# Modulation sums on VectorE, half of the low parts by adding DMAs, and values transposed, in a transformer layer

## The chip, the cores and the metric

The kernel runs on one core of a Trainium2 chip. The metric is the time of one execution on the device in microseconds (us), as the median of three runs.

## What is computed

One layer for 512 tokens of width 2048, all in fp32: a modulation of norms and residuals by a vector c, a mixer of eight attention heads (each query keeps 128 keys, picked by an index score) and sixteen RWKV-7 heads, an output projection, and a gated feed-forward of width 5632.

```python
mod = silu(c) @ w_ada + b_ada
sh1, sc1, gt1, sh2, sc2, gt2 = split(mod, 6)
h = rms_norm(x, norm1_g) * (1 + sc1) + sh1
proj = h @ w_in
mixed = concat([attention(proj[..., :4176]), rwkv7(proj[..., 4176:])]) @ w_out
x = x + gt1 * mixed
h2 = rms_norm(x, norm2_g) * (1 + sc2) + sh2
x = x + gt2 * ((silu(h2 @ w_gate) * (h2 @ w_up)) @ w_down)
```

## The kernel before

**Products.** Activations lie transposed, features on the 128 partitions and tokens along the row, as tiles of 128x512. A large product is made of three, to keep fp32 accuracy: each operand is split into a rounded high part and a low part (what is left), and high x high, high x low and low x high are added up in PSUM.

**Weight stream.** All large products form one list of jobs. A job is one chunk of weights of 512 KB, loaded into `wraw` (three buffers), split in two halves into `whi` and `wlo` (four buffers each, 128x512), and used by 24 products of 128x512. ScalarE makes the high part by a copy into the rounded type, `split` then has the low part made by a subtraction. In the middle section of the list (`state["mid"]`, 110 jobs from the rest of the input projection's groups up to the output projection, about 155 to 1130 us) every second low part is made by GpSimd, the others by VectorE. `split_to` puts the splits of a chunk into the queues about one and a half chunks ahead of its products.

**Side work.** Everything else is written as generators that yield, and `drive` lets each go a step further after every third product, so that side work is laid between the products in TensorE's queue. Whether a step is ready is judged by a rough clock kept while the program is written (`clk`, one entry for each queue): `until` waits for that clock to pass the time at which a tile should be there, `room` for a queue's backlog to be small. On the chip each engine takes its queue in order; if an operand is later than the rough clock thought, TensorE stands still.

**RWKV.** `prep` (line 650), once for each of eight pairs of heads, makes decays and scaled keys with a chain on VectorE from the scan `L` to the tile `work`; `work` is stored, transposed by TensorE into the PSUM tile pT, and the values `vt` are turned into token-major form in the PSUM tile pV by products with the identity. Both are copied into `pack` by ScalarE, four chunks of 64 tokens in each of two halves, and stored. `solve` (line 779) solves the triangular systems of four pairs at a time, one problem on each partition; the first four on GpSimd, the second four on VectorE. A scan over the chunks and the attention heads follow.

**Modulation.** The first third of `mod` (shift and scale of the first norm) is made at the start. `ada_stream` (line 966) makes the other four vectors gt1, sh2, sc2 and gt2, each in four blocks of 512 columns: for each of 16 rows of blocks of w_ada a 256 KB tile `wad` comes in, ScalarE multiplies it by the column of silu(c), GpSimd adds it to the block's sum, and `ada_sum` adds up over the partitions. There are 256 such tiles; from the last four of the output projection's column tiles until the first gate tile the last vector's tiles are held back (`state["rest"]`). The output projection's end needs gt1, the second norm sh2 and sc2, the down projection gt2.

Of the kernel before, what the change touches and what calls it, by code (L numbers as in the profile page):

```python
# [8 lines left out]
F32 = mybir.dt.float32  # L9
# [9 lines left out]
KD = D // 128  # L19
# [21 lines left out]

# columns of the constant table
C_ID, C_MASK, C_CAUS, C_BLKM = 0, 128, 256, 384
# [5 lines left out]
def layer_kernel(ctx, tc, x, c, positions, w_ada, b_ada, norm1_g, w_in, q_norm_g, k_norm_g,  # L49
# [5 lines left out]

    # A rough clock for each queue, kept while the program is written: it decides when side work joins the queues.
    clk = dict(pe=0.0, dve=0.0, act=0.0, pool=0.0, dma=0.0)
# [77 lines left out]

    SLACK = 0.5

    def until(*aps):
        """let the products run on until what these hold is there."""
        t = max(ready.get(nm(a), 0.0) for a in aps) + SLACK  # L140
        while now() < t:
            yield
# [5 lines left out]
    def banks(n):  # L148
        """wait for n free banks of the side pool."""
        while True:  # L150
            for k in [k for k, v in psread.items() if v is not None and v <= now()]:
                del psread[k]
            if len(psread) + n <= 4 and side["pe"] <= SIDE:
                return
            yield
# [42 lines left out]

    # ---------------------------------------------------------------- constants
    cst = const.tile([128, C_W], F32, name="cst")  # L200
# [27 lines left out]

    # ---------------------------------------------------------------- weight stream
    jobs = []  # L230
    subs = []
    state = {"issued": 0, "split": 0, "mid": False, "rest": False}

    def job(view, k0, nk, c0, ncols, mms, need=None, before=None, after=None, whole=False):
        """a chunk of weights, with the products that use it; its two halves are split one by one."""
        j = dict(view=view, k0=k0, nk=nk, c0=c0, n=ncols, mms=mms, need=need, before=before, after=after, i=len(jobs),
                 hi=[], lo=[], s0=len(subs), whole=whole)
        jobs.append(j)
        subs.extend([(j, u) for u in range(min(nk, 2))])
# [9 lines left out]
    def split_to(n):  # L249
        while state["split"] < min(n, len(subs)):  # L250
            j, u = subs[state["split"]]
            if j["i"] >= state["issued"]:
                return
            h = max(1, j["nk"] // 2)
            hi = wpool.tile([128, 512], F32R, name="whi", tag="whi", bufs=4)
            lo = wpool.tile([128, 512], F32R, name="wlo", tag="wlo", bufs=4)
            hv, lv = (t[:, 0:h * j["n"]].rearrange("p (k m) -> p k m", m=j["n"]) for t in (hi, lo))
            split(hv, lv, j["raw"][:, u * h:(u + 1) * h], P if state["mid"] and state["split"] % 2 else V)
            j["hi"] += [hv[:, i, :] for i in range(h)]
            j["lo"] += [lv[:, i, :] for i in range(h)]  # L260
            state["split"] += 1
# [38 lines left out]
    def group_T(view, c0, mts, klist, kc, rhs, evac, pool=PG, need=None, before=None, kneed=None, add=True, chunk_done=None, apart=False):  # L300
        """out^T tiles: mts = [(column offset, M)], contracted over klist in chunks of kc."""
        box = {}
# [31 lines left out]

    # ---------------------------------------------------------------- inputs
    xtok = [[hpool.tile([128, 512], F32, name="xtok", tag="h") for _ in range(4)] for _ in range(NT)]
# [16 lines left out]

    # scale and shift, some columns at a time; the loads run as far ahead as there is room
    BLOCKS = [(0, 1), (1, 1)] + [(k, 2) for k in range(2, KD, 2)]
# [38 lines left out]

    # rms of x, and x transposed
    ssq = SM("ssq")
# [12 lines left out]

    # vectors as columns  # L410
    v1 = const.tile([128, 128], F32, name="v1")
# [25 lines left out]
    def tables():  # L437
        """cos and signed sin of the rotary angles, features on partitions."""
        pos = G("pos", I32)
# [32 lines left out]

    # first group: the loras and two tiles of k, as the columns of h come
    first = []
# [47 lines left out]

    # ---------------------------------------------------------------- modulation, first part
    def colsum(dst, t):
        """column 32 b + c of t, summed over the partitions of a quarter, to partition c of the quarter and column b."""
        u = G("tr")
        V.transpose(u, t)
        V.tensor_reduce(dst, u.rearrange("p (b c) -> p b c", c=32), axis=mybir.AxisListType.X, op=OP.add)

    def spread(ps, parts, col=C_MOD):  # L530
        """the quarters added up: the sum of column 128 j + q to partition q and column j."""
        pv = parts.rearrange("p (j a) -> p a j", a=4)
# [60 lines left out]

    # ---------------------------------------------------------------- rwkv: evacuation with token shift
    def shifted(ps, M, mcol, name):
# [33 lines left out]

    # scratch in DRAM  # L630
    pk = dram.tile([NC, 128, PAIRS, 512], F32, name="pk")
# [18 lines left out]
    def prep(j):  # L650
# [77 lines left out]
        for half in range(2):  # L728
# [4 lines left out]
            pV = PS("pV")  # L733
            for cc in range(4):
                cI = half * 4 + cc
                mm(pV[64:128, cc * 128:(cc + 1) * 128], vt[:, cI * C:(cI + 1) * C], ident)
            yield
            A.copy(pack[half][:, :, 256:384], pT.rearrange("p (c f) -> p c f", f=128))
            A.copy(pack[half][64:128, :, 384:512], pV[64:128].rearrange("p (c f) -> p c f", f=128))
            yield from banks(2)  # L740
# [34 lines left out]

    # ---------------------------------------------------------------- rwkv: triangular solve, one problem per partition
    solved = set()
# [42 lines left out]

    # ---------------------------------------------------------------- rwkv: chunk scan over all heads
    mix = {}
    scanned = set()

    def scan(g):
        """the pairs of a group, chunk after chunk."""
        while g not in solved or done["prep"] < PAIRS:
# [131 lines left out]

    # ---------------------------------------------------------------- modulation, second part  # L960
    mod = {n: const.tile([128, 16], F32, name=n) for n in ("gt1", "sh2", "sc2", "gt2")}
# [4 lines left out]
    def ada_stream():  # L966
# [11 lines left out]

        nl = ns = 0
        acc = None  # L980
        for i, (bi, k) in enumerate(chunks):
            while state["rest"] and bi >= 12:
                yield
            while nl < i + (4 if 0 not in mix else 2):
                load(nl)
                nl += 1
            while ns < min(i + 2, nl, len(chunks)):
                t = tiles[ns]
                if ns > i and ready[nm(t)] > now():
                    break  # L990
                yield from until(t)
                A.activation(t, t, AF.Copy, scale=ccol(chunks[ns][1]))
                ns += 1
            t = tiles.pop(i)
            if k == 0:
                acc = t
                continue
            yield from until(t)
            yield from room("pool", 1.0 if 0 < done["prep"] - 3 and 0 not in solved else 2.5)
            P.tensor_tensor(acc, acc, t, op=OP.add)  # L1000
            if k == KD - 1:
                start(ada_sum(acc, *blocks[bi]))
# [17 lines left out]

    # ---------------------------------------------------------------- attention
    iwt = const.tile([128, NT, 16], F32, name="iwt")
# [142 lines left out]

    # the four query tiles of a head share three banks
    PLACE = {3: (0, 0), 2: (1, 0), 0: (1, 384), 1: (2, 0)}
# [63 lines left out]

    # ---------------------------------------------------------------- the main stream of products
    ALLK = list(range(KD))
# [38 lines left out]

    # out projection, contracted over the rwkv half first
    mT = {}
# [34 lines left out]
    def evac_out(m0):  # L1309
        def f(ps, which=(0, 1)):  # L1310
            for i in which:
                m, p = m0 + i, ps[i]
                state["rest"] = m >= KD - 4
                t = xres.pop(m)
# [21 lines left out]
    for m in range(4, KD, 2):  # L1336
        group_T(wout, m * 128, TWO, KO, 4, mixed, evac_out(m), kneed=kneed, before=load_x([m, m + 1]),
                apart=m == KD - 2)
    # the column sums of the squares need every tile
    i_norm2 = len(jobs)  # L1340
# [3 lines left out]
    def norm2():  # L1344
# [15 lines left out]
        A.copy(rb2, prb)  # L1360
        att["rb2"] = rb2

    def h2make(k):
# [7 lines left out]

    # feed-forward, in parts of its width
    gate = {}
# [3 lines left out]
    def evac_gate(f0):  # L1377
        def f(ps):
            state["rest"] = False
            for i in range(2):  # L1380
# [41 lines left out]

    # gate and up together in the first group, as the columns of h2 come
    gbox, ubox = {}, {}
# [26 lines left out]

    # ---------------------------------------------------------------- go
    start(run_rb())
# [106 lines left out]
```

## Time and profile before

| | |
|---|---|
| time, median of 3 runs | 2809.06 us (2808.62 to 2809.23) |
| profiled execution | its span of 2808.0 us; no other time of it is listed |
| instructions | 35665 |
| mean granted TensorE clock | 0.975 |

The profile shows one execution, taken by the hardware profiler. PE is TensorE's products, PEld its weight loads, DVE VectorE, ACT ScalarE, POOL GpSimd, SP SyncE, which issues most DMAs. Every line of a group has the number L127, as all operations pass one helper; so groups are told apart by their tiles, written as output<-inputs. A granted clock of 1.00 stands for the upper of TensorE's two levels (2.4 GHz), the lower one is half of it. An fp32 product that is not split is listed as two records, a transpose as one.

### The profile page before, as it was taken

The numbers are of one execution on the slowest core, as the hardware profiler recorded it, in microseconds if no ns is written. First come the engines' busy times: TensorE is split into PE (matmuls) and PEld (weight loads), VectorE is DVE, ScalarE is ACT, GpSimd is POOL, SyncE is SP. The second block draws the span as 40 slices with busy tenths as digits, with TensorE's granted clock in tenths as the row PEclk, the third lists the DMA queues.
The fourth block names the chain that finished last, engine by engine and source line by source line (L and its number), as shares of the span: only waits on it lengthen the run. The fifth ranks groups of instructions, "written<-read, shape, count | busy, mean of one in ns | idle before, by whom it ended". The sixth has DMA issues, their size and how long they took to land.

```text
span 2808.0 us, 35665 instructions
## 1 busy us (share of the span) xinstructions
PE 2699.7 (96%) x13439; PEld 2131.3 (76%) x13439; DVE 1362.6 (49%) x2064; ACT 953.0 (34%) x1691; POOL 801.9 (29%) x695
## 2 busy tenths in 40 slices
PE   7998988988999999999799999999999999999999
PEld 4576766667677768788688888888888888888887
DVE  4476445588957875743743233232333323333333
ACT  3255542332333335554452222222222222222222
POOL 2057768974434566654340000000000000000000
PEclk8999999989999999999899999999999999999999
DMA  9976765355466434464253333323333333333233
GB/s 324 312 243 202 227 184 146 103 131 174 149 198 195 137 128 136 156 220 149 77 193 98 98 98 97 97 95 96 97 98 98 98 98 98 98 98 95 93 101 110
DMA packets 383580, 396.12 MB, mean 141 GB/s; under 512 B 52442, under 2 KB 332832, under 8 KB 383408
## 3 DMA queue, kind: packets, MB, share of 16 engines
q1 hardware_dynamic: 381312, 387.78, 44.5%
q0 software_dynamic: 1952, 5.81, 0.6%
q8 instruction: 105, 1.72, 0.3%
q14 instruction: 67, 0.55, 0.1%
q10 hardware_dynamic: 144, 0.26, 0.0%
HBM read 358.13 MB, written 35.65 MB: 140 GB/s over the span
## 4 chain that ended last, share of the span: by engine, by line
PE 81%; DVE 9%; DMA 4%; POOL 2%; issue 2%; ACT 1%; SPq 1%; DVEq 0%; ACTq 0%; POOLq 0%
PE acc L127 71%; DMA wraw<-in_w_in_dram 2%; PE p L127 1%; DVE X L127 1%; PE po L127 1%; DVE stmp L127 1%; PE vacc L127 1%; DVE work L127 1%; DVE wlo L127 1%; SPq L127 1%; PE adaacc L127 1%; DMA wada<-in_w_ada_dram 1%; DVE score L127 1%; PE pV L127 1%; DVE u L127 0%
## 5 line engine op out<-in xcount | busy, mean ns | idle before, releaser
L127 DVE TENSOR_TENSOR wlo<-wraw,whi 128x512 fp32r<-128x512 f32 (+2 forms) x750 | 553.2, 743 | 1111.3 <-ACT whi L127 1104.8
L127 ACT CAST whi<-wraw 128x512 fp32r<-128x512 f32 (+2 forms) x860 | 517.9, 607 | 1251.9 <-PE acc L127 1085.7
L127 PE MATMUL acc<-hhi,whi 128*128 128x512 f32 (+1 forms) x2256 | 914.4, 405 | 4.4 <-ACT hhi L127 4.0
L127 PE MATMUL acc<-hhi,wlo 128*128 128x512 f32 (+1 forms) x2256 | 887.2, 393 | 19.2 <-DVE wlo L127 15.5
L127 PE MATMUL acc<-hlo,whi 128*128 128x512 f32 (+1 forms) x2256 | 886.2, 393 | 3.6 <-DVE hlo L127 3.6
L127 PEld LDWEIGHTS acc<-hhi,whi 128*128 128x128 f32 (+1 forms) x2256 | 425.2, 188 | 128.4 <-issue 32.4
L127 PEld LDWEIGHTS acc<-hhi,wlo 128*128 128x128 f32 (+1 forms) x2256 | 426.0, 189 | 116.3 <-DVE wlo L127 19.3
L127 PEld LDWEIGHTS acc<-hlo,whi 128*128 128x128 f32 (+1 forms) x2256 | 426.3, 189 | 95.4 <-DVE hlo L127 6.4
L127 PE MATMUL acc<-act,whi 128*128 128x512 f32 x1408 | 434.8, 390 | 0.0
L127 POOL TENSOR_TENSOR wad<-wad 128x512 f32<-128x512 f32 x240 | 343.0, 1429 | 150.5 <-ACT wad L127 139.0
L127 PEld LDWEIGHTS acc<-act,whi 128*128 128x128 f32 x1408 | 263.2, 188 | 53.8
L127 PE MATMUL acc<-act,wlo 128*128 128x512 f32 x704 | 274.0, 389 | 0.0
L127 POOL TENSOR_TENSOR wlo<-wraw,whi 128x512 fp32r<-128x512 f32 (+1 forms) x110 | 157.9, 1436 | 235.4 <-ACT whi L127 223.9
L127 ACT ACTIVATE wad<-wad,cact 128x512 f32<-128x512 f32 x256 | 179.0, 719 | 14.4 <-DMA wad<-in_w_ada_dram 14.1
L127 PEld LDWEIGHTS acc<-act,wlo 128*128 128x128 f32 x704 | 132.1, 188 | 27.6
L127 PE MATMUL acc<-mhi,whi 128*128 128x512 f32 x256 | 100.5, 392 | 0.0
L127 PE MATMUL acc<-mhi,wlo 128*128 128x512 f32 x256 | 99.7, 389 | 0.0
L127 PE MATMUL acc<-mlo,whi 128*128 128x512 f32 x256 | 99.6, 389 | 0.0
L127 DVE SCALAR_TENSOR_TENSOR x<-acc,gt,x 128x512 f32<-128x512 f32 x80 | 57.3, 750 | 41.6 <-PE acc L127 41.6
L127 POOL TENSOR_TENSOR X<-X,stmp 128x504 f32<-128x504 f32 (+33 forms) x69 | 67.0, 970 | 5.4
L127 POOL TENSOR_TENSOR stmp<-X,N 128x504 f32<-128x504 f32 (+33 forms) x69 | 63.7, 923 | 4.6 <-DVE work L127 1.4
L127 PE MATMUL vacc<-whi,hhi 128*128 128x512 f32 x128 | 58.1, 454 | 0.0
(257 smaller groups left out, 2328.5 us busy)
## 6 DMA issues: line engine op xcount, KB each, us to landing
wad<-in_w_ada_dram SPq DMA_DIRECT2D x256, 256.0 KB, 4.4
wraw<-in_w_in_dram SPq DMA_DIRECT2D x108, 512.0 KB, 5.0
wraw<-in_w_ffn_down_dram SPq DMA_DIRECT2D x88, 512.0 KB, 3.4
wraw<-in_w_ffn_gate_dram SPq DMA_DIRECT2D x84, 512.0 KB, 3.5
wraw<-in_w_ffn_up_dram SPq DMA_DIRECT2D x84, 512.0 KB, 3.4
wada<-in_w_ada_dram SPq DMA_DIRECT2D x128, 256.0 KB, 6.7
wraw<-in_w_out_dram SPq DMA_DIRECT2D x32, 512.0 KB, 3.5
pk<-pack SPq DMA_DIRECT2D x16, 768.0 KB, 3.8
```

The source lines that it names most:

```text
L127: return f(*args, **kw)
```

## The change

- **Modulation's second part.** ScalarE scales only the first of a block's 16 tiles. The other 15 are multiplied and added in one instruction on VectorE (240 in all, `scalar_tensor_tensor`, both tensors in SBUF). A step comes not before 4.2 us by the rough clock after the last one (3.0 us for the last vector), and loads run three tiles ahead at most. The last vector's tiles wait until the second norm is done (`state["ffn"]`), so they run beside the feed-forward; `state["rest"]` is gone.
- **Low parts.** In the middle section every second low part, which GpSimd made, comes about in another way: ScalarE writes the negated high part into `wlo`, and a DMA issued by GpSimd reads the same 256 KB of weights from DRAM again and adds them to it.
- **Values transposed.** In `prep`, per half, four products of 64 columns with the identity become two transposes of 128 columns; the copies into `pack` are two instead of one, each with every second chunk.

The lines of the diff that only drop a comment are left out.

```diff
+    PACE, PACE2 = 4.2, 3.0
...
-    state = {"issued": 0, "split": 0, "mid": False, "rest": False}
+    state = {"issued": 0, "split": 0, "mid": False, "ffn": False}
...
-            split(hv, lv, j["raw"][:, u * h:(u + 1) * h], P if state["mid"] and state["split"] % 2 else V)
+            if state["mid"] and state["split"] % 2:
+                A.copy(hv, j["raw"][:, u * h:(u + 1) * h])
+                A.activation(lv, hv.bitcast(F32), AF.Copy, scale=-1.0)
+                P.dma_start(lv, j["view"][:, j["k0"] + u * h:j["k0"] + u * h + h, j["c0"]:j["c0"] + j["n"]],
+                            accum_op=OP.add)
+            else:
+                split(hv, lv, j["raw"][:, u * h:(u + 1) * h])
...
             pV = PS("pV")
-            for cc in range(4):
-                cI = half * 4 + cc
-                mm(pV[64:128, cc * 128:(cc + 1) * 128], vt[:, cI * C:(cI + 1) * C], ident)
+            for i in range(2):
+                tb = half * 2 + i
+                PE.transpose(pV[:, i * 128:(i + 1) * 128], vt[:, tb * 128:(tb + 1) * 128], ident)
             yield
             A.copy(pack[half][:, :, 256:384], pT.rearrange("p (c f) -> p c f", f=128))
-            A.copy(pack[half][64:128, :, 384:512], pV[64:128].rearrange("p (c f) -> p c f", f=128))
+            for odd in range(2):
+                A.copy(pack[half][64:128, odd::2, 384:512], pV[odd * 64:odd * 64 + 64, 0:256].rearrange("p (i f) -> p i f", f=128))
...
-        nl = ns = 0
+        nl = 0
         acc = None
+        last = 0.0
         for i, (bi, k) in enumerate(chunks):
-            while state["rest"] and bi >= 12:
+            while bi >= 12 and not state["ffn"]:
                 yield
-            while nl < i + (4 if 0 not in mix else 2):
+            while nl < min(i + 3, 192 if bi < 12 else 256):
                 load(nl)
                 nl += 1
-            while ns < min(i + 2, nl, len(chunks)):
-                t = tiles[ns]
-                if ns > i and ready[nm(t)] > now():
-                    break
-                yield from until(t)
-                A.activation(t, t, AF.Copy, scale=ccol(chunks[ns][1]))
-                ns += 1
             t = tiles.pop(i)
+            while now() < last + (PACE if bi < 12 else PACE2):
+                yield
+            yield from until(t)
+            yield from room("dve", 2.0)
+            last = now()
             if k == 0:
+                A.activation(t, t, AF.Copy, scale=ccol(0))
                 acc = t
                 continue
-            yield from until(t)
-            yield from room("pool", 1.0 if 0 < done["prep"] - 3 and 0 not in solved else 2.5)
-            P.tensor_tensor(acc, acc, t, op=OP.add)
+            V.scalar_tensor_tensor(acc, t, ccol(k), acc, op0=OP.mult, op1=OP.add)
...
-                state["rest"] = m >= KD - 4
...
         att["rb2"] = rb2
+        state["ffn"] = True
...
-            state["rest"] = False
```

## Rows read from the trace of the kernel before

**Rows 1.** The page's part 1: busy us, share of the span, instructions.

```profile
PE 2699.7 (96%) x13439; PEld 2131.3 (76%) x13439; DVE 1362.6 (49%) x2064; ACT 953.0 (34%) x1691; POOL 801.9 (29%) x695
```

**Rows 2.** By stretch: length, busy PE PEld DVE ACT POOL, clock, DMA share, GB/s.

```profile
200.00:400.00 200.00, 177.68 (x909) 135.83 (x908) 110.09 (x119) 98.18 (x164) 147.86 (x110) 0.94 0.71 215
400.00:600.00 200.00, 176.33 (x871) 128.86 (x870) 118.24 (x135) 61.66 (x113) 166.21 (x160) 0.91 0.44 122
600.00:800.00 200.00, 183.25 (x976) 134.98 (x975) 167.27 (x238) 64.20 (x122) 91.26 (x85) 0.91 0.61 170
...
1360.00:1380.00 20.00, 17.91 (x69) 14.33 (x70) 17.90 (x28) 7.21 (x15) 7.23 (x5) 0.86 0.26 79
1400.00:1620.00 220.00, 220.00 (x978) 181.94 (x977) 77.51 (x108) 79.13 (x131) 34.03 (x26) 1.00 0.39 129
```

**Rows 3.** Waits of PE in 200:400, 400:600, 600:800: us, times, longest.

```profile
PE pT L127 <- DVE work L127: 21.1, 4, 5.9
...
PE pT L127 <- DVE work L127: 15.1, 3, 7.1
...
PE acc L127 <- DVE wlo L127: 7.1, 3, 3.7
```

**Rows 4.** DVE in order of time, 305 to 345: start, duration, operation.

```profile
313.38 2.32 DVE L127 TENSOR_TENSOR_SCAN L<-reset,sg 128x512 f32<-128x512 f32 x1
...
322.18 1.75 DVE L127 TENSOR_TENSOR at<-at,e 128x512 f32<-128x512 f32 x1
...
325.52 1.74 DVE L127 TENSOR_TENSOR work<-kf,e 128x512 f32<-128x512 f32 x1
```

**Rows 5.** Operations on the tile ang: count, ns least/median/most, first and last start.

```profile
L127 DVE SCALAR_TENSOR_TENSOR ang<-nrot,ang x8: 681/1666/1775, 163.0 to 183.6; 128x512 f32<-128x512 f32 x8
```

**Rows 6.** POOL in order of time, 305 to 345.

```profile
312.83 1.79 POOL L127 TENSOR_TENSOR wlo<-wraw,whi 128x512 fp32r<-128x512 f32 x1
...
328.36 6.13 POOL L127 TENSOR_TENSOR wad<-wad 128x512 f32<-128x512 f32 x4
```

**Rows 7.** PE in order of time, 318 to 340; in brackets the wait before.

```profile
327.32 1.11 PE L127 MATMUL pT<-cst,work 128*128 128x128 f32 x4 [5.03 <-DVE work L127]
328.37 1.97 PE L127 MATMUL pV<-cst,v 128*64 128x128 f32 x8
...
333.63 0.60 PE L127 MATMUL pT<-cst,work 128*128 128x128 f32 x4
334.16 1.09 PE L127 MATMUL pV<-cst,v 128*64 128x128 f32 x8
335.18 0.50 PE L127 MATMUL acc<-hhi,whi 128*128 128x512 f32 x1
```

**Rows 8.** Groups of instructions in 155:1130: busy us, mean ns, idle before.

```profile
L127 POOL TENSOR_TENSOR wad<-wad 128x512 f32<-128x512 f32 x161 | 232.8, 1446 | 38.3 <-ACT wad L127 30.3 <-PE vacc L127 2.2
L127 POOL TENSOR_TENSOR wlo<-wraw,whi 128x512 fp32r<-128x512 f32 (+1 forms) x108 | 154.6, 1432 | 235.3 <-ACT whi L127 223.9 <-PE pst L127 11.1
L127 ACT CAST whi<-wraw 128x512 fp32r<-128x512 f32 (+1 forms) x217 | 131.8, 615 | 242.4 <-DMA wraw<-in_w_in_dram 103.8 <-PE acc L127 102.6 <-PE vacc L127 23.4
L127 ACT ACTIVATE wad<-wad,cact 128x512 f32<-128x512 f32 x174 | 120.9, 719 | 14.4 <-DMA wad<-in_w_ada_dram 14.1
```

**Rows 9.** By stretch: the solve's stmp (DVE, POOL), then PE's products with whi.

```profile
400.00:450.00 50.00, 0.00 (x0) 27.85 (x36) 0.97 0.46 127
...
150.00:200.00 50.00, 44.90 (x147) 1.00 0.81 278
...
1050.00:1100.00 50.00, 36.73 (x117) 1.00 0.39 127
...
155.00:1130.00 975.00, 572.06 (x1716) 0.95 0.56 169
```

**Rows 10.** DMA issues: KB each, median us from issue to landing.

```profile
wad<-in_w_ada_dram SPq DMA_DIRECT2D x256, 256.0 KB, 4.4
...
wraw<-in_w_in_dram POOLq DMA_DIRECT2D x7, 256.0 KB, 6.3
```

## Prediction

> **What bounds the kernel now.** First the page's head: TensorE is busy 96% of the 2808.0 us, VectorE 49%, ScalarE 34%, GpSimd 29% [rows 1]. Time can only be won where TensorE waits or runs at the lower clock, or by giving TensorE less to do.
>
> Next the busy time by stretch [rows 2], to see where the missing 4% lie. TensorE lacks 22.3 us in 200 to 400, 23.7 in 400 to 600 and 16.8 in 600 to 800, with a mean granted clock of 0.94, 0.91 and 0.91; in the feed-forward from 1400 on it is full at 1.00. All that the change touches, except the last vector, lies between 155 and 1130 us.
>
> Then the waits of TensorE [rows 3]. Up to 600 us nearly all is one wait: the transposes pT wait for VectorE's `work`, 21.1 us in four waits and then 15.1 in three. From 600 to 800 the largest is for low parts from VectorE, 7.1.
>
> Last, one such wait in order of time. VectorE's chain from `L` at 313.38 to the last `work` ends at 327.26 [rows 4]. Five of its operations have two inputs in SBUF, 128x512 or 128x504, and take 1.64 to 1.77 us each (two of them are shown); a multiply-add of this size takes 0.68 us at its shortest, with a median of 1.67 [rows 5]. GpSimd works without a gap through just that time, making `wlo` and adding up `wad`; the first and the last of six such groups are shown [rows 6]. On TensorE [rows 7] the wait is 5.03 us, and what follows runs at the lower of the clock's levels: four transposes take 1.11 us where the next four take 0.60, the eight pV records 1.97 where the next eight take 1.09.
>
> **The change part by part.**
>
> *Values transposed.* Each half of a pair has eight pV records now; from pV to the next product is 1.02 us at full clock (334.16 to 335.18), against 0.53 from four pT to pV (333.63 to 334.16) [rows 7]. Two transposes should thus take 0.27 us: 0.75 saved, 16 times, 12.0 us of TensorE. Part of it may fall into a wait, so the bounds are 0 and 12.0; I take 12.0, since this work stands behind the wait, not in it. ScalarE's one evacuation becomes two of half the length; if each took a cast's 0.62 us [rows 8], that would be 10 us more in all on an engine that is busy 98 of 200 us at most here [rows 2]: hidden.
>
> *Vector sums on VectorE.* Gone are ScalarE's scaling of `wad` (0.72 us each) and GpSimd's adds (1.45 us each) [rows 8]; 240 multiply-adds with two SBUF inputs come to VectorE, and 16 scalings stay. One costs 0.68 us alone and up to 1.77 against GpSimd [rows 5]; with GpSimd's two big readers gone I take 0.7. At one in 4.2 us or more that is 33 us in 200, hidden wherever VectorE has that room: it has 90, 82 and 33 us free in the three stretches [rows 2]. Where it has not, all of it delays the chain.
>
> Between 200 and 400 GpSimd's readers were these two, so the chain's five slow operations fall from about 1.71 to 0.69: 5.1 us less, as long as the wait was (5.03); `L`, 2.32 us beside GpSimd, should fall too and pay for one multiply-add in between. So I let the waits of this stretch go, 22.3 us, and with each of the four the slow work behind it, about 2.1 us (1.11 less 0.60, 1.97 less 1.09, some 0.7 in the products after): 30.7 in all. Bounds: 15, if half stays, and 34, if the clock recovers wholly (6% of 200 us).
>
> Between 400 and 600 the first solve runs on GpSimd, 27.9 us of the first 50 [rows 9], and goes on reading SBUF. What leaves GpSimd here is a fifth of the 154.6 us of low parts, 31 us [rows 8]; what comes to VectorE is 33 us. The chain then gains little: I take 5 us, between a loss of 21 (the 15.1 us of waits doubled, and 6 of slow clock) and a gain of 30 (all 23.7 idle, and 6 of clock).
>
> Between 600 and 800 the second solve is on VectorE, slowed by GpSimd's `wad` and `wlo`. Against 33 us more stand most of GpSimd's 91 us, gone [rows 2]. I take half of the 16.8 us idle, with some clock 9; bounds 0 and 23. Next late there is the scan, which goes from TensorE to ScalarE and VectorE and back.
>
> A rule bears on this. The Trainium skill, "SBUF — State Buffer", section "Who interferes with whom", says that a VectorE operation with two SBUF inputs and a GpSimd operation that reads SBUF shut each other out for the whole instruction. The two durations of one form agree with it. By it the new multiply-adds, which have two such inputs, would collide with the first solve too; the 400 to 600 stretch would come out at its bad bound, and the sum 26 us higher. That is the second rival below.
>
> *Low parts by adding DMAs.* Some 108 low parts leave GpSimd, 1.43 us each [rows 8]. Each becomes a second pass of ScalarE (I take the cast's 0.62; 67 us in all, where nearly all of 121 us of scaling leaves [rows 8]) and a DMA from GpSimd that adds 256 KB of weights from DRAM. Queued behind it on GpSimd are the small operations of `prep` and the solve, and VectorE's `L` waits for some of those; before, they stood behind the low part itself, so they lose nothing unless the issue takes longer than 0.8 us (1.43 less 0.62). No adding DMA is in this trace. Nearest rows: GpSimd's 256 KB loads landed after 6.3 us, SyncE's 256 KB `wad` after 4.4 [rows 10]. I take 6.3, the same engine and size, with bounds of 4.4 and, as an adding DMA reads its target too, twice 6.3, 12.6. From the release of its buffer a low part is then there after 0.62 + 0.62 + 0.3 for handing over + 6.3 = 7.8 us.
>
> What it may take follows from the four buffers: half chunk n reuses that of n-4, so it has the one and a half chunks between the two. Sixteen products of a chunk use `whi`. The 147 of them in 150 to 200 are a chunk per 5.4 us, 8.2 us of room; the 117 in 1050 to 1100 one per 6.8, 10.3 of room; over the whole 975 us, 1716 are one per 9.1, 13.6 of room [rows 9]. At 6.3 it fits by 0.4 us in the densest stretch, and where the DMAs are busier it won't: I take 10 us. At 4.4 nothing is late. At 12.6 it takes 14.1, and a chunk can't be faster than (14.1 + 2.7)/2 = 8.4 us, or 95 such products in 50 us: 27 us are lost in the first of those windows (50 x 147/95 less 50), 12 in the other, and, as the rest is as uneven around its mean, I put the whole at twice that, 80.
>
> By the Trainium skill ("DMA: Bandwidth & Descriptors", "Anatomy of one DMA") a GpSimd DMA takes 2.0 us plus its bytes at 436 GB/s: an estimate of 2.6 us for 256 KB. The measured 6.3 is far above it; by the page this term would be 0 and the sum 10 us lower.
>
> *Last vector in the feed-forward.* Sixty multiply-adds at 3 us or more run from about 1390 on, where VectorE is busy 78 of 220 us and TensorE full [rows 2]: hidden. Only at the start is VectorE busy 17.9 of 20 us; five of them there may cost 0 to 5, and I take 2. The first down product wants the vector: 64 steps of 3.3 us (the pace is looked at every third product) are 211 us, and the gate and up products before it some 260 (48 chunks of 5.4), so the cover is 50 us.
>
> **Sum.** -12.0 - 30.7 - 5 - 9 + 10 + 2 = -44.7. The profiled execution spans 2808.0 us, 1.1 below the median of the runs, 2809.06: 2764.4, say 2764.
>
> **The rivals.**
>
> *Adding DMAs land late.* The other side. It decides from a landing of about 11.5 us on, where the loss nears the 54.7 us won elsewhere; at 12.6, -54.7 + 80 = +25, 2834. For it: 6.3 is a plain load. Against it: those loads ran beside the first burst of inputs, while the DMA engines' share is 0.44 to 0.71 here [rows 2].
>
> *Contention stays.* First solve and multiply-adds slow each other: 400 to 600 loses 21, 600 to 800 gains nothing: -12.0 - 30.7 + 21 + 10 + 2 = -9.7, 2799. For it: VectorE fills 118 of 200 us there, and 47 multiply-adds of 1.7 would be 80 more. Against it: the program's clock holds them back while VectorE is behind.
>
> *All waits go.* -12.0 - 34 - 30 - 23 + 0 + 2 = -97, 2712. For it: one cause stands behind most of them. Against it: the first solve still reads SBUF.
>
> **How the numbers follow.** My forecast has 0.52, with a range of its own of 2735 to 2793; late landing 0.20, contention 0.14, all gone 0.14. Over 0.2%, 5.6 us, can be told from no change here. Faster: 0.52 + 0.14 + 0.09 of contention = 0.75. Same: 0.04 of contention and 0.02 of late landing. Slower: 0.18 and 0.01, 0.19. Eight in ten takes in most of both neighbours: 2722 to 2816.
>
> **What would show it.** Right: two pV records a half, VectorE's chain from `L` to `work` near 8 us before 400, no pT wait of 5 us there, a granted clock of 0.98 or more, adding DMAs that land within 7 us. Wrong: over 30 us of TensorE waiting for `wlo` from a DMA; pT waits as long as before after 400; TensorE idle at the first down products.

## The result, and the profile after

The changed kernel takes 2832.97 us (median of 4 runs, 2832.56 to 2835.93) beside 2808.84 for the kernel before on the same chip: a ratio of 1.009 (95% interval 1.0075 to 1.0104), 24 us slower. Forecast were 2764 and a range of 2722 to 2816. The profiled execution took 2832.56 and spans 2830.8 us. Of the rivals, late adding DMAs (2834) has the right time, but at a landing half of the one it asked for, and as only one of two causes.

The page's head, for [rows 1]: GpSimd has lost 364 us of work and VectorE gained 34, as meant, and TensorE has 21 us less to do in a span that is 23 longer.

```profile
PE 2678.4 (95%) x13343; PEld 2116.4 (75%) x13343; DVE 1396.9 (49%) x2304; ACT 877.0 (31%) x1577; POOL 438.1 (15%) x455
```

By stretch, in the columns of [rows 2], with 800 to 1000 added:

```profile
200.00:400.00 200.00, 185.18 (x936) 142.84 (x935) 99.75 (x155) 83.86 (x147) 58.48 (x64) 0.96 0.84 208
400.00:600.00 200.00, 165.45 (x790) 120.70 (x789) 140.56 (x155) 69.78 (x131) 158.13 (x151) 0.89 0.69 170
600.00:800.00 200.00, 188.53 (x1188) 142.52 (x1187) 136.92 (x268) 66.36 (x129) 37.58 (x52) 0.97 0.84 204
800.00:1000.00 200.00, 193.00 (x1283) 144.06 (x1282) 150.58 (x314) 63.84 (x119) 58.45 (x56) 1.00 0.65 171
```

TensorE's idle time fell by 7.5 us in 200 to 400 and by 5.3 in 600 to 800, and rose by 10.9 in 400 to 600. In 800 to 1000 it was 0.95 us before (the line below) and is 7.0 now.

```profile
800.00:1000.00 200.00, 199.05 (x1431) 150.87 (x1430) 152.22 (x319) 70.84 (x134) 93.34 (x85) 1.00 0.54 166
```

The waits of TensorE, for [rows 3], in 200:400, 400:600, 600:800, 800:1150 and 1150:1400:

```profile
PE acc L127 <- DMA wlo<-in_w_in_dram: 12.1, 4, 6.8
...
PE pT L127 <- DVE work L127: 1.1, 1, 1.1
...
PE acc L127 <- DMA wlo<-in_w_in_dram: 15.9, 5, 5.6
PE pT L127 <- DVE work L127: 12.3, 3, 7.1
...
PE acc L127 <- DMA wlo<-in_w_in_dram: 6.8, 2, 6.6
...
PE pl L127 <- DVE s L127: 6.7, 1, 6.7
...
PE pc L127 <- DVE part L127: 27.2, 1, 27.2
```

Two large waits are new. In the middle, products wait for a low part that a DMA has still to add to: 45.7 us in 15 waits by the page's groups. At the second norm, TensorE waits once, 27.2 us, for the sum of a modulation vector (`pc` from `part`); the kernel before has no such wait. (The smaller one for `s` is taken up with e11.)

Two marks split the time, the first product of the output projection (`acc` from `mhi` and `whi`) and the second norm's first product (`pst` from `ssum`):

| kernel | output projection starts | second norm | span |
|---|---|---|---|
| before | 1147.4 | 1337.8 | 2808.0 |
| after | 1147.4 | 1362.2 | 2830.8 |

All of the 24 us that the norm comes later lie between the marks: the middle section gained and lost the same, and from the norm to the end it is 1470.2 and 1468.6 us. Why the norm is late is seen in the multiply-adds' own windows (VectorE's operations on `wad`: length, busy time, clock, DMA share, GB/s):

```profile
600.00:800.00 200.00, 10.83 (x14) 0.97 0.84 204
800.00:1000.00 200.00, 20.75 (x28) 1.00 0.65 171
...
1150.00:1200.00 50.00, 7.29 (x9) 1.00 0.43 146
1200.00:1250.00 50.00, 8.44 (x10) 1.00 0.49 165
1250.00:1300.00 50.00, 8.48 (x10) 1.00 0.51 173
```

At nine in 50 us, about what the last three show, the 192 steps of the first three vectors need some 1070 us, and from the first at 171 there are 1170 until the norm of before. But 600 to 800 has 14 operations in place of some 36, 22 too few, 120 us of pace; 800 to 1000 with 28 is behind too, by less. VectorE had the time: it is idle for 63 of these 200 us. The steps were not issued. Three holds in the loop can do that, all by the rough clock: the pace of 4.2 us, `until` for the loaded tile, and `room`, which looks at VectorE's backlog. Which of them held back most, no run shows.

The two-input operations did what was forecast where GpSimd was quiet. VectorE from `L` to the last `work`, for [rows 4], and TensorE's pT and pV of a half, for [rows 7]:

```profile
312.35 1.22 DVE L127 TENSOR_TENSOR_SCAN L<-reset,sg 128x512 f32<-128x512 f32 x1
...
317.30 0.69 DVE L127 TENSOR_TENSOR work<-kkn,at 128x512 f32<-128x512 f32 x1
317.91 0.69 DVE L127 TENSOR_TENSOR work<-kf,e 128x512 f32<-128x512 f32 x1
```

```profile
349.21 0.60 PE L127 MATMUL pT<-cst,work 128*128 128x128 f32 x4
349.65 0.38 PE L127 MATMUL pV<-cst,v 128*128 128x128 f32 x2
349.79 0.48 PE L127 MATMUL acc<-hhi,whi 128*128 128x512 f32 x1
```

The chain takes 6.2 us where it took 13.9, and pV 0.14 to the next product, where it took 1.02. The new multiply-adds (operations on `wad`, as in [rows 5]: least/median/most in ns) cost 0.745 us in 300:400 and 1.38 in 400:500, beside the first solve on GpSimd:

```profile
L127 DVE SCALAR_TENSOR_TENSOR wad<-wad,cact x15: 742/745/1777, 299.3 to 399.0; 128x512 f32<-128x512 f32 x15
...
L127 DVE SCALAR_TENSOR_TENSOR wad<-wad,cact x14: 740/1382/2252, 399.0 to 489.3; 128x512 f32<-128x512 f32 x14
```

By the Trainium skill, "SBUF — State Buffer", section "Who interferes with whom", a VectorE instruction with two SBUF inputs and a GpSimd instruction that reads SBUF contend for a shared port, which is an exclusive lock. These two rows agree with it.

The adding DMAs, by groups in 155:1130 (for [rows 8]: count, busy us, mean ns, idle before) and by DMA issues (for [rows 10]):

```profile
L127 POOL DMA_DIRECT2D wlo<-in_w_in_dram x107 | 124.1, 1160 | 449.6 <-ACT wlo L127 358.0 <-PE acc L127 39.4 <-ACT R L127 20.3
...
L127 ACT ACTIVATE wlo<-whi 128x512 fp32r<-128x512 f32 x106 | 67.0, 632 | 3.4
```

```profile
wad<-in_w_ada_dram SPq DMA_DIRECT2D x256, 256.0 KB, 3.9
...
wlo<-in_w_in_dram POOLq DMA_DIRECT2D x107, 256.0 KB, 5.4
```

They land after 5.4 us (3.8 to 10.1), less than the 6.3 of the forecast, and are late all the same. What GpSimd mostly waits for before it issues one is ScalarE's negated high part (358.0 of 449.6 us); a release by TensorE makes up 39.4. One case follows: first ScalarE in order of time, then a piece of the chain of waits (start, us, what), last TensorE's product behind it:

```profile
280.06 1.14 ACT L127 CAST whi<-wraw 128x512 fp32r<-128x512 f32 x2 [7.18 <-DMA wraw<-in_w_in_dram]
281.23 0.63 ACT L127 ACTIVATE wlo<-whi 128x512 fp32r<-128x512 f32 x1
```

```profile
282.17 7.92 DMA wlo<-in_w_in_dram
290.08 0.04 issue
290.12 2.07 PE acc L127 x4
```

```profile
290.12 0.79 PE L127 MATMUL acc<-hhi,wlo 128*128 128x512 f32 x1 [3.37 <-DMA wlo<-in_w_in_dram]
```

ScalarE stood 7.18 us because the chunk of weights had not come. From that arrival the low part took two casts, the negation, the issue and the landing: 10.0 us, 280.06 to 290.08. VectorE's subtraction of the other half of this chunk began at 280.71 and took 0.69. Weights are one start of this path and not the only one: over the whole section ScalarE's casts waited 151.5 us for weights and 172.5 for TensorE, which still used a buffer of `whi`:

```profile
L127 ACT CAST whi<-wraw 128x512 fp32r<-128x512 f32 (+1 forms) x217 | 132.0, 617 | 349.2 <-PE acc L127 172.5 <-DMA wraw<-in_w_in_dram 151.5 <-PE vacc L127 24.7
```

### The profile page after: what moved, and what is told of

It is laid out like the page before. It is cut to its first block, busy times and chain, and to the rows that moved or that the text cites. A ratio compares the mean times of both kernels' runs of the same rounds, so it can differ in the third digit from the quotient of the medians.

```text
span 2830.8 us, 35243 instructions
## 1 busy us (share of the span) xinstructions
PE 2678.4 (95%) x13343; PEld 2116.4 (75%) x13343; DVE 1396.9 (49%) x2304; ACT 877.0 (31%) x1577; POOL 438.1 (15%) x455
## 4 chain that ended last, share of the span: by engine, by line
PE 79%; DMA 7%; DVE 5%; issue 4%; SPq 2%; ACT 1%; POOL 1%; POOLq 0%; DVEq 0%; ACTq 0%
PE acc L127 68%; DMA wlo<-in_w_in_dram 3%; PE vacc L127 3%; DMA wraw<-in_w_in_dram 2%; PE po L127 2%; SPq L127 2%; PE p L127 2%; PE adaacc L127 1%; DMA wada<-in_w_ada_dram 1%; DVE work L127 1%; PE pl L127 1%; DVE wlo L127 1%; DVE score L127 1%; PE dot L127 0%; DMA xtok<-in_x_dram 0%
## 5 line engine op out<-in xcount | busy, mean ns | idle before, releaser
L127 DVE TENSOR_TENSOR wlo<-wraw,whi 128x512 fp32r<-128x512 f32 (+2 forms) x750 | 517.5, 695 | 1106.8 <-ACT whi L127 1097.5
L127 PE MATMUL acc<-hhi,wlo 128*128 128x512 f32 (+1 forms) x2256 | 892.8, 396 | 51.1 <-DMA wlo<-in_w_in_dram 45.7
L127 POOL DMA_DIRECT2D wlo<-in_w_in_dram x109 | 126.6, 1161 | 451.0 <-ACT wlo L127 359.2
L127 DVE SCALAR_TENSOR_TENSOR wad<-wad,cact 128x512 f32<-128x512 f32 x240 | 195.1, 813 | 1.2
L127 POOL TENSOR_TENSOR stmp<-X,N 128x504 f32<-128x504 f32 (+33 forms) x69 | 71.1, 1031 | 3.3
L127 ACT ACTIVATE wlo<-whi 128x512 fp32r<-128x512 f32 (+1 forms) x110 | 69.2, 629 | 3.5
L127 POOL TENSOR_TENSOR X<-X,stmp 128x504 f32<-128x504 f32 (+33 forms) x69 | 68.8, 997 | 5.4
```

Of the source, the lines that this page charges most:

```text
L127: return f(*args, **kw)
```

## The experiments

Each diff is against the changed kernel unless it says otherwise. The table has both marks, the median and the ratio to the kernel before, measured beside it on the same chip.

| run | output projection | second norm | median us | ratio (95%) |
|---|---|---|---|---|
| e1_pace30 | 1159.6 | 1351.5 | 2822.8 | 1.0052 (1.0035 to 1.0069) |
| e2_no_adding | 1129.9 | 1342.4 | 2810.1 | 1.0005 (0.9995 to 1.0014) |
| e3_pv_only | 1144.8 | 1334.6 | 2806.64 | 0.9996 (0.9987 to 1.0005) |
| e4_adding_only | 1196.2 | 1387.8 | 2862.29 | 1.0207 (1.0173 to 1.0241) |
| e6_pace_out_no_adding | 1126.3 | 1320.0 | 2790.39 | 0.9932 (0.9917 to 0.9947) |
| e7_pace_out | 1148.5 | 1339.3 | 2810.6 | 1.0005 (0.9996 to 1.0015) |
| e8_plain_copy | 1127.5 | 1342.4 | 2814.18 | 1.0017 (1.0005 to 1.0029) |
| e9_copy_no_wait | 1093.2 | 1310.5 | 2779.53 | 0.9893 (0.9878 to 0.9909) |
| e10_vec_only | 1130.7 | 1324.3 | 2793.7 | 0.9948 (0.9933 to 0.9963) |
| e11_hold_topk | 1108.4 | 1301.1 | 2770.71 | 0.9866 (0.9849 to 0.9882) |
| e13_low_on_vector | 1129.2 | 1321.0 | 2789.27 | 0.9931 (0.9916 to 0.9946) |
| e14_slow_in_solve | 1094.6 | 1285.6 | 2754.89 | 0.9808 (0.9792 to 0.9824) |

**A faster pace everywhere (e1_pace30).**

```diff
-    PACE, PACE2 = 4.2, 3.0
+    PACE, PACE2 = 3.0, 3.0
```

> The changed kernel with a pace of 3.0 in place of 4.2 for the first twelve blocks. My theory: the changed kernel loses about 24 us at the second norm, where TensorE stands 27.2 us because the sum of sc2 isn't finished, and about as much in the middle section as it wins there. Then this one comes out near 2809 (2833 less 24), and its norm starts right after the output projection. The rival: the multiply-adds themselves load VectorE too much, and a faster pace only moves the loss into the middle section: 2820 to 2835.

2822.8, in the rival's range. The wait at the norm is gone, but the output projection starts 12.2 us later, so about half of what is saved at the norm is lost before it. That the denser multiply-adds are what costs there is the rival's account; this run alone doesn't show it.

**The change without adding DMAs (e2_no_adding)**, and **adding DMAs alone on the kernel before (e4_adding_only)**: the same lines taken out of the one and put into the other.

```diff
-            if state["mid"] and state["split"] % 2:
-                A.copy(hv, ...)
...
+            split(hv, lv, j["raw"][:, u * h:(u + 1) * h], P if state["mid"] and state["split"] % 2 else V)
```

> The changed kernel with the low parts as before (every second one by GpSimd's subtraction), all else as changed. My theory: TensorE's 45.7 us of waits for adding DMAs, with the slow clock behind them, go and little comes in their place: 2833 less 40 to 60, 2773 to 2793. The rival: the adding DMAs cost little (they land after 5.4 us, sooner than I assumed), and the gain in the middle was eaten by multiply-adds on VectorE beside GpSimd's reads: 2825 to 2840.

> The kernel before with every second low part of the middle section by an adding DMA and nothing else. My theory: late low parts cost 45 us or more, and GpSimd, still adding up the modulation, issues them later still: 2835 to 2870. The rival, adding DMAs cost little: 2800 to 2815, as VectorE gets faster beside an emptier GpSimd.

Without them the kernel takes 2810.1, outside both ranges: no gain over before, but 23 us less than with them. Alone they cost 54 us (2862.29 beside 2808.01), in the expected range, though TensorE waits no longer for `wlo` there than in the changed kernel (41.6 us beside 45.7); what makes them dearer on the kernel before is not shown. In e2 the wait at the norm stays, 24.0 us, and a new one of 14.5 shows at 1000 us (below); so two causes are there, and the adding DMAs are only one of them.

**Transposed values alone on the kernel before (e3_pv_only).** The diff's pV lines alone.

> The kernel before with the values transposed and nothing else. By the predicted term, 12.0 us of TensorE go: 2797. The rival: the work falls into the waits for VectorE's chain, and nothing is left of it: 2807 to 2811.

2806.64, 0.4 us below the rival's range: what it says held. In 155 to 1130 TensorE is busy 887 us where it was 907, its waits there add up to 88.0 us where they were 67.9, and the projection starts 2.6 us earlier: the time saved became waiting.

**The hurried end (e7_pace_out, and e6_pace_out_no_adding with the low parts as before).** Once the middle section is over, a step comes every 1.2 us.

```diff
-            while now() < last + (PACE if bi < 12 else PACE2):
+            while now() < last + ((PACE if state["mid"] else 1.2) if bi < 12 else PACE2):
```

> The changed kernel with low parts as before and, once the middle section is over, a pace of 1.2 in place of 4.2 for the first twelve blocks. My theory: with the run of the changed kernel without adding DMAs, all that stood between it and a gain was TensorE's 24.0 us at the second norm, and the output projection, where VectorE is 44% busy and TensorE full, hides the faster steps: 2810 less 24, 2783 to 2790. The rival: as with a pace of 3.0 throughout, what is won at the norm is half lost elsewhere: 2797 to 2805.

> The changed kernel, adding DMAs and all, with a pace of 1.2 after the middle section for the first twelve blocks. My theory: 24 us of the norm go and the middle section stays as it is, level with the kernel before: 2806 to 2812; the difference to the same kernel without adding DMAs is their price, 17 to 25. The rival: 2818 to 2826, as with a pace of 3.0.

My account held in both, with e6 0.4 us above its range. The late sums cost 22.4 us with adding DMAs (2832.97 to 2810.6) and 19.7 without (2810.1 to 2790.39); the norm comes 191 to 194 us after the first mark, as in the kernel before. e6 beats both kernels. The adding DMAs cost 20.2 us here, and by the first mark 22.2.

**What in the adding DMA costs (e8_plain_copy, e9_copy_no_wait).** Both make half the low parts the weights themselves.

```diff
 # e8: the DMA copies, ScalarE's negation stays
-                            accum_op=OP.add)
 # e9: also no negation, so the DMA waits for its buffer alone
-                A.activation(lv, hv.bitcast(F32), AF.Copy, scale=-1.0)
```

> The changed kernel with the DMAs for low parts copying the weights in place of adding them (the low parts are then the weights themselves, negation still made before). My theory: the adding isn't what costs; landing stays above 4.5 us (5.4 with adding), TensorE waits 35 to 50 us for these DMAs, time 2825 to 2835. The rival, adding is the price: landing under 4 us, waits under 20, time 2805 to 2818.

> As the copying variant, but with the negation left out too, so that the DMA waits for its buffer alone and no more for the weights and ScalarE (the low parts are the weights themselves). My theory: what lacked was the time from the landing of the weights on, not from the release of the buffer: waits of TensorE for these DMAs fall below 15 us, time 2805 to 2820. The rival, DMAs from GpSimd are too slow for the four buffers whatever they wait for: waits of 30 us or more, 2825 to 2835.

e8 gave the rival's time, 2814.18, but neither account whole: 30.0 us of waits for `wlo` stay, and the landing is 4.5 us. So adding in place of copying costs 19 us; each DMA lands 0.9 us later with it and occupies GpSimd 0.44 us longer. The copy, in the same order behind ScalarE, still comes late. The rows of e8 (the DMA's group, its issues, TensorE's wait):

```profile
L127 POOL DMA_DIRECT2D wlo<-in_w_in_dram x109 | 77.9, 715 | 467.3 <-ACT wlo L127 398.0 <-PE acc L127 26.6 <-ACT R L127 19.9
...
wlo<-in_w_in_dram POOLq DMA_DIRECT2D x107, 256.0 KB, 4.5
...
PE acc L127 <- DMA wlo<-in_w_in_dram: 30.0, 12, 5.9
```

e9 took a further 34.6 us off, more than expected. Its rows, the DMA's group and TensorE's wait:

```profile
L127 POOL DMA_DIRECT2D wlo<-in_w_in_dram x108 | 77.3, 716 | 364.7 <-PE acc L127 220.3 <-PE vacc L127 95.5 <-DMA wlo<-in_w_in_dram 14.2
```

```profile
PE acc L127 <- DMA wlo<-in_w_in_dram: 1.8, 2, 1.3
```

At a median landing of 4.6 us, with up to 9.6, and with DMA engines as full as in e8 (0.79 and 0.77 in 200 to 400), hardly any DMA is late if it may start when its buffer comes free: TensorE's waits for them fall from 30.0 to 1.8 us. So it is not the landing by itself that makes them late, but what they stand behind, the weights' arrival and ScalarE. ScalarE's 67 us of negations are gone in e9 too; what they cost by themselves was not tried, so the 34.6 us are the price of both together.

**Transposed values in the new setting (e10_vec_only).** e6 with the old pV products.

> The second modulation part on VectorE with the hurried end, low parts as before, and the values' 64 products again in place of the 32 transposes: of the change only the multiply-adds and the last vector are left. Mine: the values' transposes gave nothing when they stood alone, because the time saved became waiting, and here the pairs run under the same multiply-adds; 2788 to 2796, at most 5 over the same kernel with the transposes (2790.4). Rival: with the waits of 200 to 400 us gone, the transposes' 12 us on TensorE reach the end: 2799 to 2806.

2793.7, in the expected range, 3.3 us above e6, with the first mark 4.4 us later. The two intervals of the ratio overlap, so no gain by the transposes is clear of noise here either; the rival's range, from 2799 on, was reached by no run of e10.

**No multiply-adds during the top-k rounds (e11_hold_topk).** In e6 TensorE waited once for 14.5 us near 1000 us; the line of e6, and TensorE's stretch 950:1000 in e6 and then in e11:

```profile
1006.49 2.93 PE L127 MATMUL pl<-k,q 128*128 128x384 f32 x6 [14.53 <-DVE s L127]
```

```profile
950.00:1000.00 50.00, 29.68 (x151) 21.27 (x147) 48.45 (x110) 6.35 (x11) 14.29 (x13) 0.83 0.34 105
```

```profile
950.00:1000.00 50.00, 39.19 (x193) 29.65 (x187) 42.10 (x106) 11.62 (x29) 16.01 (x17) 0.86 0.28 85
```

VectorE is nearly full there in e6 (48.45 of 50 us). The edit, against e6:

```diff
+            while done["idx"] and not done["topk"]:
+                yield
```

> The hurried end, low parts as before, and no multiply-add issued between the index scores and the end of the top-k rounds (they are made up behind the last in-projection). Mine: TensorE's 14.5 us for a head's sum s, near 1000 us, comes of VectorE carrying the rounds and the multiply-adds together; that wait is gone or under 3 us, and the time 2774 to 2784. Rival: the rounds alone fill VectorE, or the work that is put off comes back before the second norm: 2787 to 2800, with a wait of 5 us or more in one of the two places.

2770.71, 20 us better than e6, a little under the range; the wait for `s` is gone and the norm does not wait for sums. So the multiply-adds made a wait of their own in the middle section, and the prediction had none there. In the changed kernel it is 6.7 us long, as its row above shows, so the 20 us are its price without adding DMAs.

**All low parts on VectorE (e13_low_on_vector).** e6 with GpSimd's subtractions given to VectorE.

> The hurried end, and all low parts by VectorE's subtraction: GpSimd makes none, and nothing adds by DMA. It asks whether the low parts had to leave VectorE at all in this kernel. Mine: 70 subtractions of about 1 us more on VectorE, which already holds the multiply-adds, make TensorE wait longer for transposed keys at 400 to 600 us and for sums at 950 to 1010: 2795 to 2815. Rival: GpSimd's subtraction held weights back and took VectorE's port: 2778 to 2790.

2789.27: no different from e6 (2790.39), so my account fell, and the rival's range, which just takes it in, says no more for its own. With the sums gone from GpSimd, the time is the same whichever of the two engines subtracts. The first solve on GpSimd is shorter without the low parts, 176 us where e6 has 218, but the waits for `work` in 400 to 600 hardly are, 17.6 us where e6 has 18.8.

**Few multiply-adds beside the first solve (e14_slow_in_solve)**, against e11:

```diff
-    PACE, PACE2 = 4.2, 3.0
+    PACE, PACE2 = 2.4, 3.0
...
-            while now() < last + ((PACE if state["mid"] else 1.2) if bi < 12 else PACE2):
+            while now() < last + ((12.0 if done["prep"] >= 4 and 0 not in solved else PACE if state["mid"] else 1.2) if bi < 12 else PACE2):
```

> As the version held during the top-k rounds (2770.7), and while GpSimd runs the first solve a multiply-add comes only every 12 us of the rough clock; before and after it every 2.4 instead of 4.2, to make up for it. It asks whose the waits of 400 to 600 us are. Mine: the multiply-adds and the first solve slow each other, so with a third of them there the solve takes under 212 us (218 with them, 207 in the kernel before), TensorE's wait for the transposed keys' source in 400 to 600 falls from 18.8 to under 12, and the time is 2758 to 2768. Rival: the solve alone slows the pairs' chain, which it did before the change too (15.1 us of waits): 15 us or more of them stay and the solve stays at 215 or more, and the time is 2768 to 2780.

2754.89, better than either theory's range, and 1.9% (1.8 to 2.1) faster than the kernel before. My account of it fell. TensorE's wait for `work` in 400:600, and GpSimd's solve:

```profile
PE pT L127 <- DVE work L127: 18.6, 4, 6.0
```

```profile
L127 POOL TENSOR_TENSOR stmp<-X,N x69: 257/948/1517, 371.4 to 585.8; 128x270 f32<-128x270 f32 x3, 128x462 f32<-128x462 f32 x3, 128x62 f32<-128x62 f32 x2, 128x120 f32<-128x120 f32 x2
```

With 9 multiply-adds in this stretch where e11 has 25, the waits stay (19.2 in e11) and the solve lasts 214 us (218): so far it is as the rival said. Neither fewer multiply-adds here nor taking the low parts from GpSimd (e13) removes these waits; that the solve alone makes them fits, and the 15.1 us of the kernel before too, but no run is without the solve. The gain is seen in two stretches, 400 to 600 and 800 to 1000, first of e11 and then of e14:

```profile
400.00:600.00 200.00, 170.08 (x817) 124.94 (x816) 147.56 (x179) 60.91 (x119) 160.40 (x149) 0.90 0.60 166
...
800.00:1000.00 200.00, 189.13 (x1175) 142.22 (x1174) 155.67 (x350) 48.78 (x101) 58.42 (x58) 0.96 0.38 114
```

```profile
400.00:600.00 200.00, 173.82 (x844) 128.14 (x845) 135.50 (x164) 58.92 (x114) 158.30 (x152) 0.95 0.55 144
...
800.00:1000.00 200.00, 197.06 (x1215) 148.78 (x1214) 164.58 (x359) 56.54 (x115) 66.73 (x66) 0.99 0.37 110
```

TensorE works 3.7 and 7.9 us more, at a granted clock of 0.95 for 0.90 and 0.99 for 0.96. That fewer sums beside the solve did this, rather than more of them ahead of it or another order of the work behind it, is not shown.

## Why the prediction was wrong

The sum was -44.7 and the result is +24.1, 68.8 apart. By its own steps:

- **A step that was not in the sum: the first three vectors' end.** The prediction asked for a cover only for the last vector. For the first twelve blocks the sum never asked how many steps fit before the second norm, and so put this term at nothing; at one in 5.6 us, about the pace that they got behind the middle section, the margin was 100 us, and one stretch alone lost 120. It cost 19.7 (e2 to e6) to 22.4 us (after to e7).
- **Low parts by adding DMAs, +10.** The landing was guessed well, 5.4 for 6.3. The failed step is the room: "From the release of its buffer a low part is then there after 0.62 + 0.62 + 0.3 for handing over + 6.3 = 7.8 us", set against the one and a half chunks that a buffer has. The release of its buffer is not what it starts from: GpSimd waits for ScalarE, and ScalarE for weights or for a buffer of `whi`. The term measured 20 us (e6 to e7) to 23 (e2 to after), and 54 alone on the kernel before. By e8 and e9, 19 is the price of adding in place of copying, and 35 that of the order behind ScalarE together with the negations. The two make more than the 23, as e9 makes no low part at all: it is 31 us faster than e2, which subtracts.
- **Late landing as a rival** had the time by luck: it asked for a landing of 11.5 us, and 5.4 sufficed. It set a loss of 80 against gains of 54.7; these DMAs cost 20 to 23, the norm's wait as much again, and the gains mostly failed to come.
- **Values transposed, -12.** The work went from TensorE, 0.88 us a half where 0.75 was worked out; the time gave 1.4 us of it in e3 and 3.3 between e10 and e6, neither clear of noise. The step that failed is "this work stands behind the wait, not in it": what came after it waited longer.
- **200 to 400, -30.7.** The mechanism was right: the chain's slow operations fell to 0.69 us, and the pT waits from 21.1 to 1.1. (The chain has six operations with two inputs in SBUF, not five: `work` from `r` and `sg` took 0.68 us before as well.) But 12.1 us of waits for adding DMAs stand in their place. Without those (e6) 10.8 us of pT waits stay; there the first solve begins at 365, within the stretch. So the size was wrong: of the 22.3 us idle 7.5 went (10.0 in e6), and the clock rose from 0.94 to 0.96, not to the 0.98 named as the sign.
- **400 to 600, -5.** Worse, as the contention rival had it: TensorE lacks 10.9 us more in after and 5.9 more in e6, which has no adding DMA (170.47 busy). The price is that rival's only in part: with a third of the multiply-adds there (e14) the pT waits are as long.
- **600 to 800, -9.** Idle time fell by 5.3 us and the clock rose from 0.91 to 0.97: right, and rather undersized. It was had with 14 multiply-adds in the stretch, 10.8 us of VectorE, where 33 us were counted.
- **800 to 1010.** No term, and a wait there: multiply-adds beside the top-k rounds, 6.7 us of wait in after, and 20 us of time by e6 and e11.
- **The last vector in the feed-forward, +2.** Right or a little high: from the norm to the end the kernel is 1.6 us shorter than before, and TensorE is full in 1420 to 1700.

By the Trainium skill, "DMA: Bandwidth & Descriptors", section "Anatomy of one DMA", a 256 KB GpSimd DMA was estimated at 2.6 us. Here the copying ones of e8 took 4.5 (median) and the adding ones 5.4, so the measurement decides; by that rule the term would have been 0, further off still.

## What to carry to other kernels

When work moves to an engine that has room, ask for each result when its last piece must be done, at the pace it will really get, and make room where that engine is a bottleneck for others: here the same multiply-adds, with the low parts as before, left the kernel as slow as it was or made it 55 us faster (e2, e14) by nothing but when they run. A load that must wait for a computed value has its latency counted from that value, not from the release of its buffer. A microsecond saved on the busiest engine counts only where the work behind it was not waiting for someone else.

## What the runs showed of the hardware

An adding DMA of 256 KB from GpSimd is dearer than a copying one in two ways: the issue occupied GpSimd for 1.16 us where the copy took 0.72 (means of some 108, changed kernel and e8), and it landed after 5.4 us where the copy took 4.5 (medians of 107). In 200 to 400 the DMA engines' share was 0.84 with adding and 0.77 with copying, at 208 and 210 GB/s.
